# A hybrid decoder layer: more raw-weight buffers, background sums paced and placed anew

## The chip, the cores and the metric

The kernel runs on one core of a Trainium2 chip, in one launch. The metric is the device time of that launch in microseconds (us): the median of several executions of the same program. A profile is taken of one further execution.

## The reference

One layer on 512 tokens of width 1024, in float32. Cut to what matters here:

```python
xn = rms_norm(x, norm1_g)
proj = xn @ w_in                     # q, k, v, branch gates, conv inputs, merge gates
o_nsa = ...                          # compressed + selected + window attention
z = conv_b * conv3(conv_c * conv_x)  # short causal convolution
mixed = sigmoid(gate_a) * (o_nsa @ w_branch_a) + sigmoid(gate_b) * (z @ w_branch_b)
x = x + mixed @ w_out
h = rms_norm(x, norm2_g)
return x + square(relu(h @ w_up)) @ w_down
```

`w_up` is 1024 x 4096 and `w_down` 4096 x 1024.

## The kernel before

**Split products.** Every weight is used as a pair. ScalarE copies a raw chunk to a rounded `w_hi` (line 86), VectorE subtracts to get `w_lo` (line 88), and each product is three matmuls on TensorE (`mm3`, lines 229 to 231). The class `Weights` keeps a plan of all chunks (128 x 1024 floats, 512 KB, some smaller) in the order of use. A raw buffer (`w_raw`, three of them) is filled by a DMA on SyncE's queue (line 62). `split_step` issues the split in program order some chunks ahead of use. When a chunk is split, `load_to(ns + 2)` issues the load that reuses its buffer, so each load waits for the `w_lo` just issued, and whatever stands behind it on SyncE's queue waits too.

**Stages.** In order: the projections and attention; the merge (eight passes of four products, gates and branches); the output projection in two halves of 512 columns; and the feed-forward part in four groups, each an up stage (`up_group`) and a down stage (`st_down`). The second half of the output projection runs token chunk by token chunk (`tok_gemm` with `tok_outer`): 24 matmuls a chunk, then `o_second` (residual add, line 855; norm to `hn`, line 907), and inside the next chunk's matmuls `mid` calls `h_chunk`, which transposes `hn` on TensorE (line 917), copies it out on ScalarE and takes the remainder on VectorE (line 926).

**Feed-forward.** Each group multiplies in seven products instead of eight (block sums of the weights, in the manner of Strassen and Winograd). The products p1 to p7 of an up stage are written by `Quad`; VectorE forms the results (line 1025) and block sums (line 1069), and the pair for the down stage (line 1019). There are two such quads per group; quads 0 and 1 of the first group are interleaved, the other groups run them one after the other.

**Background sums.** The block sums of weights (`tu1` to `tu4` for an up stage, `td1` to `td4` for a down stage) are made ahead in DRAM, while other stages run. There are eight sets, `sums[0]` to `sums[7]`. `sums_by_dma` copies DRAM to DRAM on SyncE's queue (line 289), then accumulates on GpSimd's queue (line 293). `sums_by_dve` loads four pieces to buffers `z`, `oT`, `bg`, adds on VectorE (line 302, 128 x 1024) and stores (lines 305 to 316). `background(steps, pace)` hands over a list of steps, and `tick(us)` issues one each time the program's own estimate of elapsed time has grown by `pace`. Sets 0 to 2 are made by DMA at 4.95 in the first part, sets 3 to 6 by VectorE at 1.8 from the first merge pass on (100 steps), and set 7, needed in the last down stage, by DMA at 13.0 from the start of the up stage of the first group.

Of the kernel before, what the change touches and what calls it, by code (L numbers as in the profile page):

```python
# [6 lines left out]
F32 = mybir.dt.float32  # L7
# [6 lines left out]
P = 128  # L14
# [4 lines left out]
NT = S // P  # L19
# [13 lines left out]
C_ALL = 1484  # L33


class Weights:


    def __init__(self, nc, raw, hl, flat, plan):
        self.nc, self.raw, self.hl, self.flat = nc, raw, hl, flat  # L40
        self.plan = plan
        self.at = 0
        self.loaded = {}
        self.parts = {}
        self.nl = 0
        self.wide = 1 << 30
        self.home = {}
        self.step = 0
        self.ns = 0

# [15 lines left out]
    def split_step(self):  # L66


        nc, k = self.nc, self.ns
        if k >= len(self.plan):  # L70
            return
        if self.step == 0:
            self.load_to(k)
            pool = self.home.get(k, self.hl)
            hi = pool.tile([P, WMAX], F32R, name="w_hi", tag="w_hi")
            lo = pool.tile([P, WMAX], F32R, name="w_lo", tag="w_lo")
            self.parts[k] = (hi, lo)
        hi, lo = self.parts[k]
        t = self.loaded[k]
        n = t.shape[1]  # L80
        if k >= self.wide:
            v = slice(0, n)
        else:
            v = slice(0, n // 2) if self.step < 2 else slice(n // 2, n)
        if self.step % 2 == 0:
            nc.scalar.activation(hi[:, v], t[:, v], AF.Copy)  # L86
        else:
            nc.vector.tensor_tensor(lo[:, v], t[:, v], hi[:, v].bitcast(F32), ALU.subtract)  # L88
        self.step = (self.step + 1) % (2 if k >= self.wide else 4)
        if self.step == 0:  # L90
            self.loaded.pop(k)
            self.ns += 1
            self.load_to(self.ns + 2)

    def split_to(self, i):
        while self.ns <= min(i, len(self.plan) - 1):
# [7 lines left out]
def layer(tc, flat, sizes, x, cst, wck, wcv, g1, g2, out):  # L104
    nc = tc.nc
# [13 lines left out]

    top.enter_context(tc.manual_schedule())  # L120
    cp, close_cp = pool("cp")
    wraw, close_wraw = pool("wraw", 3)
    whl, close_whl = pool("whl", 4)
    xtp, close_xtp = pool("xtp")
    qkv, close_qkv = pool("qkv")
# [37 lines left out]

    xs = [sp.tile([P, DM], F32, name=f"x{c}") for c in range(NT)]
    g1b = sp.tile([P, DM], F32, name="g1b")
    cs = cp.tile([P, C_ALL], F32, name="cs")
    warm = cp.tile([P, 1], F32, name="warm")
    nc.vector.memset(warm, 1.0)
    nc.scalar.activation(warm, warm, AF.Sqrt)
# [4 lines left out]
    for b in range(2):  # L174
        nc.sync.dma_start(xs[0][:, b * 512 : b * 512 + 512], x[0:P, b * 512 : b * 512 + 512])
    nc.sync.dma_start(g1b, g1.partition_broadcast(P))
    nc.scalar.dma_start(cs[:, C_ID : C_ID + P], cst[:, C_ID : C_ID + P])
    W.load_to(1)
    load_x(1)
    W.load_to(2)  # L180
    wck_t = pre.tile([P, 16, HD], F32, name="wck_t")
    wcv_t = pre.tile([P, 16, HD], F32, name="wcv_t")

    ident = cs[:, C_ID : C_ID + P]
    junk = sp.tile([P, DM], F32, name="junk")
    st1 = cp.tile([P, NT], F32, name="st1")
    xh = xtp.tile([P, NKO, S], F32R, name="xh")
# [87 lines left out]
    for c in range(NT):  # L275
# [2 lines left out]
            v, v, q_ss[:, c, :].unsqueeze(2).to_broadcast([P, NH, HD]), ALU.mult  # L278
        )
    close_sp()  # L280
    zp, close_zp = pool("zp", side="right")
    cvp, close_cvp = pool("cvp", 2, side="right")

    def sums_by_dma(sets):

        for u in sets:
            for k, m in ((4, 0), (6, 1), (5, 2), (7, 3)):
                for h in u:
                    nc.sync.dma_start(h[k], h[m])
                    yield  # L290
            for k, m in ((4, 1), (6, 2), (5, 4), (7, 5)):
                for h in u:
                    nc.gpsimd.dma_start(h[k], h[m], accum_op=ALU.add)
                    yield
# [505 lines left out]
    for n in range(NKO):  # L800
# [20 lines left out]
        if n == 0:  # L821

            r = [t[:, k : k + 2, :].rearrange("p a t -> p (a t)") for t, k in
                 ((z, 0), (z, 2), (z, 4), (z, 6), (oT, 0), (oT, 2))]
            r += [bgp.tile([P, 1024], F32, name=f"bg{k}") for k in range(2)]
            background(sums_by_dve(sums[3:7], (r[:4], r[4:])), 1.8)
    for f in (close_gp, close_bp, close_xtp):
        f()

# [28 lines left out]
    def tok_gemm(ci, act, after, tok_outer, last=False, mid=None):  # L858
# [15 lines left out]
        else:  # L874
            for c in range(NT):
                parts = 2 if last and c == NT - 1 else 1
                for b in range(parts):
                    n = 512 // parts
                    ps = ps_acc.tile([P, 512], F32, name="acc", tag="acc")
                    for kp in range(4):  # L880
                        hi, lo = W.get(ci + kp)
                        for k in range(2):
                            ko = 2 * kp + k
                            w = slice(k * 512 + b * n, k * 512 + (b + 1) * n)
                            mm3(ps[:, :n], part(act, ko, c), (hi[:, w], lo[:, w]),
                                ko == 0, ko == NKO - 1)
                        tick(1.45 / parts)
                        if (c, kp) in ((2, 1), (2, 3), (3, 0), (3, 1)):
                            W.split_to(W.ns)
                        if kp == 2 and b == parts - 1 and c:  # L890
                            mid(c - 1)
                    if parts == 1:
                        after(c, ps)
                    else:
                        after(c, ps[:, :n], b * n, n)
# [48 lines left out]

    tok_gemm(ci + 4, (mh, ml), o_second, True, mid=o_mid)
    ci += 8
    background(sums_by_dma(sums[7:]), 13.0)
    close_wo()
    close_bgp()
    close_mp()  # L950
# [169 lines left out]
    def st_down(ci, last):  # L1120
# [30 lines left out]
        for ps, slot_, start, reads in (  # L1151
# [18 lines left out]
            else:  # L1170

                for j, o, n in ((0, 0, 512), (1, 0, 512)) if not last else (
                    (1, 0, 256), (0, 0, 512), (1, 256, 256)
                ):
                    for c in range(2):
                        ci += c
# [5 lines left out]

    for g in range(4):
        up_group(g)
        st_down(ci, g == 3)
        ci += 14
    for f in (close_gp2, close_hs, close_up, close_hp, close_ps_acc, close_ps_tr, close_ps_t, close_whl, close_wraw, close_cp, close_dr):
# [112 lines left out]
```

## Time and profile before

| quantity | value |
| --- | --- |
| median of 3 runs | 832.41 us (831.45 to 834.02) |
| the profiled execution | 837.87 us, span of the trace 836.0 us |
| TensorE busy | 798.0 us, 95% of the span, 4421 matmuls |
| VectorE busy | 585.8 us, 70% |
| ScalarE busy | 395.7 us, 47% |
| GpSimd busy | 88.5 us, 11% |
| mean granted TensorE clock | 0.988 |
| DMA, mean over the span | 206 GB/s |

The trace gives for each instruction its start from the span's begin, its duration, and the idle time of its engine just before it with the instruction that ended that idle time. An engine's name with a q (SPq, ACTq) is its queue of instructions that issue DMAs. The share of busy time is an average over stages that have different limits, so the rows below are taken by stage.

### The profile page before, as it was taken

What the parts mean: (1) busy time and instruction counts of PE and PEld (TensorE: products, weight loads), DVE (VectorE), ACT (ScalarE), POOL (GpSimd) and SP (SyncE); (2) the same over time, 40 slices, a digit from 0 to 9 for tenths busy, and PEclk for the clock granted to TensorE, in tenths of its full rate; (3) what the DMA queues carried; (4) which work ended last, traced back from release to release, by engine and by line L of the source; (5) the groups of instructions that cost most, each with busy time, mean ns of one, the idle gap of its engine ahead of it and who ended that gap; (6) DMA issues with size and microseconds to landing.
All of it is one profiled execution on the core that took longest, in us unless ns stands there. A gap on an engine that the chain in (4) does not pass through costs nothing.

```text
span 836.0 us, 11917 instructions
## 1 busy us (share of the span) xinstructions
PE 798.0 (95%) x4421; PEld 686.2 (82%) x4421; DVE 585.8 (70%) x1005; ACT 395.7 (47%) x714; POOL 88.5 (11%) x138
## 2 busy tenths in 40 slices
PE   5999989999999999999999887889989999999998
PEld 4898868888888888888888677878988899889986
DVE  6677887666666376566555677667588869967984
ACT  5454555455544362232222556663355446535641
POOL 0001553234224100000000000000000000000000
PEclk9999999999999999999999999979999999999999
DMA  8346668559568748988799654868887665565562
GB/s 311 130 124 199 131 138 201 170 129 193 158 191 169 152 154 268 336 295 267 275 319 375 242 181 135 208 197 261 247 221 204 208 204 188 179 199 190 178 221 107
DMA packets 49450, 172.56 MB, mean 206 GB/s; under 512 B 5616, under 2 KB 6000, under 8 KB 49392
## 3 DMA queue, kind: packets, MB, share of 16 engines
q1 hardware_dynamic: 43920, 152.33, 54.3%
q0 software_dynamic: 4608, 16.78, 12.9%
q10 hardware_dynamic: 864, 2.69, 0.9%
q8 instruction: 35, 0.57, 0.3%
q14 instruction: 23, 0.19, 0.1%
HBM read 152.90 MB, written 52.43 MB: 246 GB/s over the span
## 4 chain that ended last, share of the span: by engine, by line
PE 76%; DVE 10%; DMA 6%; ACT 5%; issue 2%; POOL 0%; SPq 0%; ACTq 0%; DVEq 0%; POOLq 0%
PE acc L229 14%; PE acc L230 13%; PE acc L231 13%; PE dacc L229 5%; PE dacc L230 5%; PE dacc L231 5%; DVE w_lo L88 3%; PE uacc L229 3%; PE uacc L230 3%; DMA w_raw<-w_flat 3%; PE uacc L231 3%; DMA w_raw<-tu 2%; PE ptu L685 2%; PE sc L638 2%; ACT w_hi L86 1%
## 5 line engine op out<-in xcount | busy, mean ns | idle before, releaser
L88 DVE TENSOR_TENSOR w_lo<-w_raw,w_hi 128x512 fp32r<-128x512 f32 (+3 forms) x268 | 234.1, 887 | 96.1 <-ACT w_hi L86 95.6
L86 ACT ACTIVATE w_hi<-w_raw 128x512 fp32r<-128x512 f32 (+3 forms) x268 | 201.7, 779 | 113.9 <-PE dacc L231 42.7
L229 PE MATMUL acc<-xh,w_hi 128*128 128x512 f32 x336 | 137.3, 409 | 0.0
L231 PE MATMUL acc<-xh,w_lo 128*128 128x512 f32 x336 | 131.6, 392 | 0.0
L230 PE MATMUL acc<-xl,w_hi 128*128 128x512 f32 x336 | 131.5, 391 | 0.0
L229 PE MATMUL dacc<-w_hi,uh 128*128 128x512 f32 (+1 forms) x228 | 88.2, 387 | 1.0 <-DVE x L1131 0.9
L230 PE MATMUL dacc<-w_lo,uh 128*128 128x512 f32 (+1 forms) x228 | 87.9, 386 | 0.0
L231 PE MATMUL dacc<-w_hi,ul 128*128 128x512 f32 (+1 forms) x228 | 87.9, 385 | 0.0
L231 PEld LDWEIGHTS acc<-xh,w_lo 128*128 128x128 f32 x336 | 63.1, 188 | 14.1
L229 PEld LDWEIGHTS acc<-xh,w_hi 128*128 128x128 f32 x336 | 63.2, 188 | 12.0 <-issue 3.3
L230 PEld LDWEIGHTS acc<-xl,w_hi 128*128 128x128 f32 x336 | 63.3, 188 | 7.9
L229 PE MATMUL uacc<-hA,w_hi 128*128 128x256 f32 x192 | 56.7, 295 | 9.9 <-DVE G L1025 9.9
L230 PE MATMUL uacc<-hA,w_hi 128*128 128x256 f32 x192 | 56.2, 292 | 0.0
L231 PE MATMUL uacc<-hA,w_lo 128*128 128x256 f32 x192 | 56.1, 292 | 0.0
L650 ACT ACTIVATE p<-p,nst 128x512 f32<-128x512 f32 (+2 forms) x48 | 29.6, 617 | 55.9 <-DVE nst L646 54.6
L229 PEld LDWEIGHTS dacc<-w_hi,uh 128*128 128x128 f32 x228 | 43.0, 188 | 10.4 <-issue 1.3
L231 PEld LDWEIGHTS dacc<-w_hi,ul 128*128 128x128 f32 x228 | 42.8, 188 | 8.7
L230 PEld LDWEIGHTS dacc<-w_lo,uh 128*128 128x128 f32 x228 | 43.0, 188 | 8.3
L229 PEld LDWEIGHTS uacc<-hA,w_hi 128*128 128x128 f32 x192 | 38.9, 203 | 10.6 <-DVE G L1025 6.9
L1131 DVE TENSOR_TENSOR x<-x,dacc 128x512 f32<-128x512 f32 (+1 forms) x57 | 36.7, 672 | 9.1 <-PE dacc L231 9.1
L691 DVE TENSOR_TENSOR pt<-ptu,pt 128x384 fp32r<-128x384 f32 (+1 forms) x48 | 28.8, 600 | 19.6 <-ACT pt L690 19.5
L666 POOL TENSOR_SCALAR p<-p,nst 128x512 f32<-128x512 f32 (+2 forms) x48 | 32.9, 693 | 88.3 <-DVE nst L664 43.3
(231 smaller groups left out, 1666.2 us busy)
## 6 DMA issues: line engine op xcount, KB each, us to landing
w_raw<-w_flat SPq DMA_DIRECT2D x110, 512.0 KB, 4.6
w_raw<-tu SPq DMA_DIRECT2D x32, 512.0 KB, 4.1
w_raw<-td SPq DMA_DIRECT2D x32, 512.0 KB, 4.4
tu<-w_flat SPq DMA_DIRECT2D x16, 512.0 KB, 6.1
td<-w_flat SPq DMA_DIRECT2D x16, 512.0 KB, 6.3
z<-w_flat SPq DMA_DIRECT2D x16, 512.0 KB, 6.7
tu<-w_flat POOLq DMA_DIRECT2D x8, 512.0 KB, 7.6
tu<-tu POOLq DMA_DIRECT2D x8, 512.0 KB, 9.4
```

The lines of the kernel that those rows point to most:

```text
L86: nc.scalar.activation(hi[:, v], t[:, v], AF.Copy)
L88: nc.vector.tensor_tensor(lo[:, v], t[:, v], hi[:, v].bitcast(F32), ALU.subtract)
L229: nc.tensor.matmul(ps, a[0], b[0], start=start, stop=False, **kw)
L230: nc.tensor.matmul(ps, a[0], b[1], start=False, stop=False, **kw)
L231: nc.tensor.matmul(ps, a[1], b[0], start=False, stop=stop, **kw)
L638: nc.tensor.matmul(ps[:, : b - a], QS[h][:, t], ks[h // 4][:, a:b], start=k == 0, stop=k == 1)
L650: later(1, lambda: nc.scalar.activation(p, p, AF.Exp, scale=-1.0, bias=mn, accum_out=sm))
L666: nc.gpsimd.tensor_scalar(p_of(u, k), p_of(u, k), nst[:, u % 4, 1, k : k + 1], 1.0, op0=ALU.mult, op1=ALU.mult,)
L685: nc.tensor.transpose(pt[:, n : n + P], p_of(u, c)[:, k * P : (k + 1) * P], ident)
L691: later(1, lambda: nc.vector.tensor_tensor(ptl[:, at], pt[:, :n], pth[:, at].bitcast(F32), ALU.subtract))
L1131: nc.vector.tensor_tensor(v, v, ps[:, o : o + n], op)
```

## The change

Parts of the diff, apart from names:

1. Five raw buffers instead of three, and a load depth that is 2 up to the end of the q projection and 4 from there on.
2. To make room, the table of constants `cs` moves to the pool that is freed before the merge; the identity for the transposes gets a small tile `ident`.
3. The sums on VectorE are paced at 1.55 instead of 1.8.
4. In the second half of the output projection the transposes of chunks 0 and 1 stand behind the next chunk's fourth weight chunk instead of behind its third; those of chunk 2 stay behind the third.
5. Set 7 starts after the up stage of the first group instead of before it, at 14.0 instead of 13.0, and its copies are issued on ScalarE's queue instead of SyncE's.
6. In the last product of the last group the 256-column pieces belong to the first accumulator instead of the second.

```diff
@@ class Weights
+        self.depth = 2
...
-            self.load_to(self.ns + 2)
+            self.load_to(self.ns + self.depth)
@@ layer
-    wraw, close_wraw = pool("wraw", 3)
+    wraw, close_wraw = pool("wraw", 5)
...
-    cs = cp.tile([P, C_ALL], F32, name="cs")
+    cs = qkv.tile([P, C_ALL], F32, name="cs")
+    ident = cp.tile([P, P], F32, name="ident")
...
-    nc.scalar.dma_start(cs[:, C_ID : C_ID + P], cst[:, C_ID : C_ID + P])
+    nc.scalar.dma_start(ident, cst[:, C_ID : C_ID + P])
...
     close_sp()
+    W.depth = 4
...
-    def sums_by_dma(sets):
+    def sums_by_dma(sets, copy=nc.sync.dma_start):
...
-                    nc.sync.dma_start(h[k], h[m])
+                    copy(h[k], h[m])
...
-            background(sums_by_dve(sums[3:7], (r[:4], r[4:])), 1.8)
+            background(sums_by_dve(sums[3:7], (r[:4], r[4:])), 1.55)
...
-                        if kp == 2 and b == parts - 1 and c:
+                        if kp == (2 if c == NT - 1 else 3) and b == parts - 1 and c:
                             mid(c - 1)
...
-    background(sums_by_dma(sums[7:]), 13.0)
...
-                    (1, 0, 256), (0, 0, 512), (1, 256, 256)
+                    (0, 0, 256), (1, 0, 512), (0, 256, 256)
...
     for g in range(4):
         up_group(g)
+        if g == 0:
+            background(sums_by_dma(sums[7:], nc.scalar.dma_start), 14.0)
         st_down(ci, g == 3)
```

Three places show what moves.

VectorE, second half of the output projection, from the norm of token chunk 0 to the add of chunk 2 (`x` is the residual, `st` the norm's sums, `hn` the normed chunk, `hA` its transposed remainder, `oT` and `bg` buffers of the background sums). Before:

```order
L907 SCALAR_TENSOR_TENSOR hn_4086<-x_0_4077,st_4091,g2b 128x1024
L302 TENSOR_TENSOR oT<-oT,bg_3090 128x1024
L926 TENSOR_TENSOR hA_4076<-ptr,hA_4075 128x2x2x128 x2
L302 TENSOR_TENSOR bg_3090<-bg_3090,oT 128x1024
L855 TENSOR_TENSOR x_1_4078<-acc,x_1_4078 128x512
L905 TENSOR_TENSOR st_4091<-st_4091 128x1
L192 TENSOR_SCALAR st_4091<-st_4091 128x1
L194 RECIPROCAL st_4091<-st_4091 128x1
L907 SCALAR_TENSOR_TENSOR hn_4087<-x_1_4078,st_4091,g2b 128x1024
L88 TENSOR_TENSOR w_lo<-w_raw,w_hi 128x1024
```

The same place in the changed kernel, to the add of chunk 2:

```order
L909 SCALAR_TENSOR_TENSOR hn_4102<-x_0_4093,st_4107,g2b 128x1024
L928 TENSOR_TENSOR hA_4092<-ptr,hA_4091 128x2x2x128 x2
L857 TENSOR_TENSOR x_1_4094<-acc,x_1_4094 128x512
L907 TENSOR_TENSOR st_4107<-st_4107 128x1
L193 TENSOR_SCALAR st_4107<-st_4107 128x1
L195 RECIPROCAL st_4107<-st_4107 128x1
L909 SCALAR_TENSOR_TENSOR hn_4103<-x_1_4094,st_4107,g2b 128x1024
L89 TENSOR_TENSOR w_lo<-w_raw,w_hi 128x1024 x2
L928 TENSOR_TENSOR hA_4092<-ptr,hA_4091 128x2x2x128 x2
L857 TENSOR_TENSOR x_2_4095<-acc,x_2_4095 128x512
```

The adds of the sums (line 302) are gone from here; they now stand ahead of the last splits of the first half. Two `w_lo` stand ahead of the second pair of `hA`, where one stood before.

TensorE at the transposes of chunk 1 (`ptr` from `hn1`), before:

```order
L229 MATMUL acc_4354<-w_hi_4267,mh_2929 128x512
L230 MATMUL acc_4354<-w_lo_4268,mh_2929 128x512
L231 MATMUL acc_4354<-w_hi_4267,ml_2930 128x512
L917 MATMUL ptr_4380<-cs_126,hn1_4087 128x128 x4
L917 MATMUL ptr_4388<-cs_126,hn1_4087 128x128 x4
L229 MATMUL acc_4354<-w_hi_4282,mh_2929 128x512
```

and now:

```order
L230 MATMUL acc_4363<-w_hi_4294,mh_2934 128x512
L231 MATMUL acc_4363<-w_lo_4295,mh_2934 128x512
L232 MATMUL acc_4363<-w_hi_4294,ml_2935 128x512
L919 MATMUL ptr_4400<-ident_127,hn1_4103 128x128 x4
L919 MATMUL ptr_4408<-ident_127,hn1_4103 128x128 x4
L230 MATMUL acc_4423<-w_hi_4191,mh_2934 128x512
```

The transposes moved from between two weight chunks of one accumulator to the seam between the accumulators of chunk 2 and chunk 3, six matmuls later.

SyncE's queue in the up stage of the first group, before (`w_raw` are loads of weights and of their sums, `td1_3` the first copies of set 7):

```order
L62 DMA w_raw_4590<-tu1_0_89 128x1024
L62 DMA w_raw_4627<-tu4_0_92 128x1024
L62 DMA w_raw_4672<-tu2_0_90 128x1024
L289 DMA td1_3_117<-w_flat 128x1024
L62 DMA w_raw_4705<-w_flat 128x1024
L62 DMA w_raw_4739<-tu3_0_91 128x1024
```

and now:

```order
L63 DMA w_raw_4446<-tu1_0_89 128x1024
L63 DMA w_raw_4540<-tu4_0_92 128x1024
L63 DMA w_raw_4595<-tu2_0_90 128x1024
L63 DMA w_raw_4632<-w_flat 128x1024
L63 DMA w_raw_4677<-tu3_0_91 128x1024
```

The eight copies of set 7 left this queue; on ScalarE's queue they stand between splits of the first group's down stage and the second group's up and down stages.

## Rows read from the trace of the kernel before

**Rows 1.** Page, busy time by engine over the span.

```profile
PE 798.0 (95%) x4421; PEld 686.2 (82%) x4421; DVE 585.8 (70%) x1005; ACT 395.7 (47%) x714; POOL 88.5 (11%) x138
```

**Rows 2.** Windows: output projection; up 1; up 2; down 3; up 4.

```profile
core 0: us, PE busy (x) PEld busy (x) DVE busy (x) ACT busy (x) POOL busy (x), PEclk, DMA share, GB/s
440.00:460.00 20.00, 20.00 (x88) 16.05 (x87) 11.36 (x15) 5.03 (x9) 0.00 (x0) 1.00 1.01 382
493.90:552.29 58.39, 46.33 (x345) 45.50 (x344) 40.51 (x49) 36.70 (x54) 1.62 (x2) 0.88 0.66 191
...
590.59:636.00 45.41, 42.24 (x337) 41.89 (x336) 33.26 (x40) 23.08 (x29) 2.44 (x3) 0.96 0.80 229
...
714.82:752.93 38.11, 38.11 (x170) 31.55 (x169) 29.18 (x36) 17.54 (x18) 0.00 (x0) 1.00 0.58 190
752.93:793.23 40.30, 40.30 (x337) 40.30 (x336) 34.92 (x42) 24.27 (x30) 0.00 (x0) 1.00 0.55 186
```

**Rows 3.** Timeline of TensorE, 460 to 836: instructions it was idle before, in brackets.

```profile
466.73 0.50 PE L230 MATMUL acc<-w_lo,mh 128*128 128x512 f32 x1 [0.69 <-DVE w_lo L88]
472.74 1.09 PE L917 MATMUL ptr<-cs,hn 128*128 128x128 f32 x8 [0.36 <-DVE hn L907]
480.99 1.07 PE L917 MATMUL ptr<-cs,hn 128*128 128x128 f32 x8 [1.54 <-DVE hn L907]
490.41 1.12 PE L917 MATMUL ptr<-cs,hn 128*128 128x128 f32 x8 [2.74 <-DVE hn L907]
...
517.57 0.39 PE L229 MATMUL uz<-hS,w_hi 128*128 128x256 f32 x1 [4.02 <-ACT p L1001]
...
547.01 0.58 PE L229 MATMUL uacc<-hA,w_hi 128*128 128x256 f32 x1 [6.70 <-DVE G L1025]
...
826.93 0.36 PE L229 MATMUL dacc<-w_hi,uh 128*128 128x256 f32 x1 [0.87 <-DVE x L1131]
```

**Rows 4.** Timeline of VectorE in the second half of the output projection.

```profile
475.53 0.69 DVE L926 TENSOR_TENSOR hA<-ptr,hA 128x512 fp32r<-128x512 f32 x1 [0.29 <-ACT hA L925]
476.14 1.22 DVE L302 TENSOR_TENSOR bg<-bg,oT 128x1024 f32<-128x1024 f32 x1
477.27 0.68 DVE L855 TENSOR_TENSOR x<-acc,x 128x512 f32<-128x512 f32 x1
...
480.76 1.22 DVE L88 TENSOR_TENSOR w_lo<-w_raw,w_hi 128x1024 fp32r<-128x1024 f32 x1
...
486.63 0.68 DVE L855 TENSOR_TENSOR x<-acc,x 128x512 f32<-128x512 f32 x1
```

**Rows 5.** Timeline of ScalarE, then of VectorE, 535 to 547.

```profile
535.07 1.06 ACT L86 ACTIVATE w_hi<-w_raw 128x1024 fp32r<-128x1024 f32 x1 [2.93 <-DMA w_raw<-tu]
...
536.16 1.23 DVE L88 TENSOR_TENSOR w_lo<-w_raw,w_hi 128x1024 fp32r<-128x1024 f32 x1 [3.30 <-ACT w_hi L86]
...
546.27 0.68 DVE L1025 TENSOR_TENSOR G<-p,uacc 128x512 f32<-128x512 f32 x1
```

**Rows 6.** Timeline of ScalarE, up stage of the second group.

```profile
594.60 1.06 ACT L86 ACTIVATE w_hi<-w_raw 128x1024 fp32r<-128x1024 f32 x1 [4.10 <-DMA w_raw<-w_flat]
...
607.08 1.06 ACT L86 ACTIVATE w_hi<-w_raw 128x1024 fp32r<-128x1024 f32 x1 [5.32 <-DMA w_raw<-w_flat]
```

**Rows 7.** The chain that ended last, 515 to 640: start, duration, what.

```profile
524.43 10.61 DMA w_raw<-tu
...
598.37 8.60 DMA w_raw<-w_flat
```

**Rows 8.** DMA issues by line: count, KB each, median us to landing.

```profile
bg<-w_flat SPq DMA_DIRECT2D x8, 512.0 KB, 7.7
```

**Rows 9.** Timelines of the queues: issues on ScalarE's, and a copy on SyncE's.

```profile
440.56 1.83 ACTq L845 DMA_DIRECT2D x<-x_in  x4
...
517.24 0.51 SPq L289 DMA_DIRECT2D td<-w_flat  x1
```

**Rows 10.** Timeline of VectorE, first half of the output projection.

```profile
455.61 1.22 DVE L302 TENSOR_TENSOR z<-z 128x1024 f32<-128x1024 f32 x1 [0.49 <-DMA z<-w_flat]
```

More of the change, by code (lines that the diff above doesn't have):

```diff
@@ L182, in layer @@
     wcv_t = pre.tile([P, 16, HD], F32, name="wcv_t")
-    ident = cs[:, C_ID : C_ID + P]
     junk = sp.tile([P, DM], F32, name="junk")
```

## The prediction

> **What bounds the kernel now.** I read the busy shares first, then the windows stage by stage, then TensorE's idle stretches, then what each of them waited for. TensorE is busy 798 of 836 us [rows 1], so all that can be won without less work is idle or slow TensorE time. The windows say where it lies [rows 2]. An up stage does the same 336 matmuls in every group; the last takes 40.30 us with TensorE full and its clock at 1.00, the second 45.41, the first 58.39 (the latter with eight transposes more, about 1 us). The down stage of the third group takes 38.11 us for 168 matmuls of 512 columns, 0.227 us each; I use 0.23 below, and 5.5 us for 24. Earlier than 460 us, apart from the start, TensorE is idle for a few us in the attention part, which the change does not touch. The waits in the part after 460 are in [rows 3]: four in the second half of the output projection (0.69, 0.36, 1.54, 2.74), two large ones in the first up stage (4.02 and 6.70), one at the end (0.87).
>
> **The output projection.** The change takes VectorE's last four adds of the sums out of this half (1.22 us each, one is in [rows 4]) and puts the transposes of chunks 0 and 1 six matmuls (1.4 us) later. I replay it.
> - The first wait, 0.69, ends on a `w_lo` that stood behind an add of 1.22; without the add it goes.
> - Chunk 0: its transposes started at 472.74, after 0.36 of waiting [rows 3]. Its `hn` is ready 0.7 earlier now, and TensorE arrives 0.36 + 0.69 earlier but has 1.4 more to do: no wait, start at 473.0.
> - Chunk 1: in program order its add (line 855) stands behind the two `hA` of chunk 0. The second of these ended 3.48 us after the transposes began (475.53 + 0.69 - 472.74), which gives 476.5; the background add that came next [rows 4] is gone. From the add's start to the next transposes it took 3.72 us (477.27 to 480.99), so 480.2. TensorE is there at 473.0 + 0.9 for the transposes + 5.5 = 479.4. It waits 0.8 instead of 1.54, and then has nothing left of chunk 2, where before 1.4 us of it remained.
> - Chunk 2: two `w_lo` of 1.22 now stand ahead of the two `hA` (0.65 each in a row). `hn` of chunk 1 ends just before 480.2, so the add starts at about 483.9. From add to transposes it was 3.78 (486.63 to 490.41), which gives 487.6 instead of 490.41: **2.8 us** earlier. TensorE, there at 480.2 + 0.9 + 18 x 0.23 = 485.2, still waits 2.4 us.
>
> So the norm's chain over VectorE and ScalarE is late next, and not all of the 5.33 us of waiting goes. Bounds: 1.4 (if the later transposes push back the add as much as they help once more) to 5.3. I take 2.8. Further on, to 517 us, the chain from the last norm to the 4.02 us wait runs over VectorE and ScalarE and no DMA ends a wait in it; it moves as a whole, and that wait stays.
>
> **The first up stage.** TensorE's wait of 6.70 us at 547.01 ends on VectorE's line 1025, 546.27 + 0.68 [rows 3, 5]. VectorE worked from 536.16 to there almost without a break, and before that stood 3.30 us for ScalarE, which stood 2.93 us for a raw chunk [rows 5]. That chunk's load took 10.61 us [rows 7], among the copies of set 7 (the first issued at 517.24 [rows 9]) and with only two loads ahead. Now four loads are ahead and set 7 starts after this stage. A load that is late by 2.93 is covered by two more chunks, each worth 24 x 0.12 = 2.9 us of TensorE's time in an up stage (40.30 / 336 = 0.12). So all 2.93 goes: **2.9 us**. The rest of the 6.70 is VectorE's own work and stays. Bounds: nothing, and 58.39 - 40.30 - 1 = 17 if all waits of the stage fell; it is near the low end because the 4.02 and the rest of the 6.70 end on compute, not on a load.
>
> **The second up stage.** ScalarE waits 4.10 and 5.32 us for raw chunks [rows 6], and a load takes 8.60 us [rows 7]. With three buffers a buffer comes round once in 8.6 + 1.06 + 1.23 = 10.9 us, 3.6 us a chunk, while TensorE uses one in 2.9. With five it is 10.9 / 5 = 2.2 us, so the stage is no longer bound by loads, even with set 7 now running beside it. Gain 45.41 - 40.30 = **5.1 us**. Bounds: nothing, and 5.1, since the last group has no such waits. I take the upper end: the loads would have to take over 12 us before five buffers don't keep up (5 x 2.9 - 2.3).
>
> **The end.** The first matmuls of the last product waited 0.87 us for the read of the second accumulator, which is read last [rows 3]. They now begin with the first accumulator, whose read is issued a half step earlier: **0.9 us**, between nothing and 0.9.
>
> **What costs nothing, and its cover.** The eight copies on ScalarE's queue hold it for 1.83 / 4 = 0.46 us each [rows 9], 3.7 us in all; ScalarE is busy 24 of 40 us in an up stage [rows 2], and the splits have the two added chunks in hand. Without that cover it is 3.7. In the Trainium skill, the page "DMA: Bandwidth & Descriptors", section "Issuing engines are not separate DMA queues", says that all queues end on the same DMA engines and that using several saves only the time to issue. By that rule the copies do not stop competing with the weights, and if they are what makes the loads late the second up stage keeps its loss (the first of the rivals). The quicker pace of the sums adds no instruction; it puts four adds more (4.9 us) ahead of the output projection's second half, where VectorE is idle 8.6 of 20 us [rows 2], and shortens the time that a load of the sums has. The constants' new place and the separate identity change no transfer on the path: 0. The deeper loads before the merge meet no wait of TensorE: 0.
>
> **Sum.** 2.8 + 2.9 + 5.1 + 0.9 = 11.7 us. The profiled execution took 837.87 us (836.0 of span and 1.9 around it), which makes 826.2. The median of the runs shown is 832.41, 5.5 below the profiled one; the waits are the same program's, so I take the 11.7 off the median: **820.7 us**.
>
> **The rivals.**
> - *The loads stay late.* The copies and the accumulations of set 7 move from the first up stage into the first down and second up stage, where they share the DMA engines with the weights, now from a second queue. For it: the share of the DMA engines is 0.80 in the second up stage and the rate only 229 GB/s, against 382 in the output projection [rows 2]. Against it: loads of 8.6 us fit five buffers. It keeps the 5.1: gain 6.6, 825.8 us.
> - *More falls than the load waits.* The four waits of the projection go altogether (2.5 more), and with shorter idle stretches the clock drops less: the mean granted clock of 0.88 in the first up stage [rows 2] is a quarter of 58 us at the 1.2 GHz level, mostly idle or just after the two long waits; 2.5 of it may come back. Gain 16.7, 815.7 us.
> - *It does not do what it says.* Every load still stands on SyncE's queue behind the `w_lo` that frees its buffer, and the sums' stores stand there too. If the order of that queue and not the depth makes the loads late, only the projection and the end win, less ScalarE's 3.7: near no change, 831 us.
> - *Slower.* The sums on VectorE starve. A buffer's next load is issued six steps before its add: 10.8 us at the old pace, 9.3 at the new. Such a load takes 7.7 us in the median [rows 8], and one was late at the old pace already, by 0.49 [rows 10]. VectorE works in order, so the splits and the gates stand behind a late add. The splits are two chunks ahead, which covers about one chunk, 5.5 us; so TensorE pays from a landing of 14.8 us on, once in each of eight jobs. Against it: the loads are far from that, and the first half of the projection gets less traffic. It decides from 14.8 + 11.7 / 8 = 16.3 us; at 17 it is 8 x 2.2 = 17.6 lost, 838.3 us.
>
> **How the numbers follow.** The forecast gets 0.62, loads that stay late 0.17, more 0.09, no change 0.07, slower 0.05. The range of 8 in 10 is 815 to 827: it takes in the two cases that lie beside the forecast and 1 us of spread around the late loads. About 0.3%, 2.5 us, is what a measurement can tell from no change. Faster by more: 0.62 + 0.17 + 0.09 = 0.88, of which I give 0.01 to no change for part gains that cancel: 0.87; within: 0.08; slower: 0.05.
>
> **What would show it.** Right: the second up stage at 40 to 41 us with no ScalarE wait for `w_raw`; in the first, one wait near 4 us as before and the second at 4 instead of 6.7; two waits for `hn` of about 0.8 and 2.4 before the feed-forward part; the first up stage begins about 3 us earlier; no wait at the last product. Wrong: loads of over 12 us in the second group, VectorE idle for `z`, `oT` or `bg` in the merge, matmuls there over 0.23 us, ScalarE idle behind its own DMA issues, or a new wait of TensorE in the first 460 us.

## The result and the profile after

The changed kernel takes 820.60 us (median of 4 runs, 819.86 to 821.24); the kernel before, on the same chip, 833.16 (831.45 to 834.02). The ratio is 0.9851, with a 95% interval of 0.9831 to 0.9872: 12.6 us less, where 11.7 were forecast, and 820.6 where 820.7 was (the forecast counts from 832.41, the median of before that was known then).

The profiled execution of the changed kernel took 820.94 us (span 819.2), close to its median; that of before took 837.87, 4.7 above its own. So the two traces differ by 16.9 us where the medians differ by 12.6, and part of what follows is how late the loads were in one execution of before. The page's line of busy shares, where TensorE goes from 95% [rows 1] to 97%:

```profile
PE 790.5 (97%) x4421; PEld 681.2 (83%) x4421; DVE 585.3 (71%) x1005; ACT 396.2 (48%) x714; POOL 88.2 (11%) x138
```

The windows that answer to [rows 2], with the same columns: the output projection, the first and second up stage, the third down stage, the fourth up stage.

```profile
440.00:460.00 20.00, 20.00 (x87) 16.10 (x86) 11.44 (x15) 5.02 (x9) 0.00 (x0) 1.00 0.95 356
489.21:543.78 54.57, 44.99 (x346) 44.38 (x345) 41.24 (x52) 36.54 (x55) 0.00 (x0) 0.91 0.44 144
581.88:621.68 39.80, 39.80 (x338) 39.79 (x337) 34.79 (x42) 24.27 (x30) 1.61 (x2) 1.00 0.91 263
699.58:737.68 38.10, 38.10 (x170) 31.54 (x169) 29.17 (x36) 17.52 (x18) 0.00 (x0) 1.00 0.60 195
737.68:777.48 39.80, 39.80 (x338) 39.79 (x337) 34.79 (x42) 24.27 (x30) 0.00 (x0) 1.00 0.56 185
```

The second up stage is full, though the DMA engines are busier there than before (0.91 against 0.80, 263 GB/s against 229). The fourth, which nothing in the change seemed to touch, is 0.5 us shorter. TensorE's idle stretches after 440 us, which answer to [rows 3]:

```profile
479.76 1.07 PE L919 MATMUL ptr<-ident,hn 128*128 128x128 f32 x8 [0.42 <-DVE hn L909]
486.91 1.06 PE L919 MATMUL ptr<-ident,hn 128*128 128x128 f32 x8 [1.89 <-DVE hn L909]
505.48 0.38 PE L231 MATMUL uacc<-hS,w_hi 128*128 128x256 f32 x1 [0.82 <-DVE hS L939]
512.52 0.47 PE L230 MATMUL uz<-hS,w_hi 128*128 128x256 f32 x1 [4.08 <-ACT p L1002]
538.79 0.58 PE L230 MATMUL uacc<-hA,w_hi 128*128 128x256 f32 x1 [4.69 <-DVE G L1026]
```

The waits of 0.69 and 0.36 in the projection and of 0.87 at the end are gone; 1.54 became 0.42, 2.74 became 1.89, 4.02 stayed (4.08), 6.70 became 4.69. ScalarE waits for no raw chunk in the second group. From the starts of the first matmuls, the stages (us, the two profiled executions):

| stage | before | after | less |
| --- | --- | --- | --- |
| output projection, to the first up stage | 55.00 | 50.18 | 4.82 |
| up 1 | 58.39 | 54.57 | 3.82 |
| down 1 | 38.30 | 38.10 | 0.20 |
| up 2 | 45.41 | 39.80 | 5.61 |
| down 2, up 3, down 3, up 4 | 157.23 | 155.80 | 1.43 |
| down 4 | 39.54 | 38.44 | 1.10 |

### The profile page after: what moved, and what is told of

Its sections match the earlier page's. It is cut to its first block, busy times and chain, and to the rows that moved or that the text cites. A ratio compares the mean times of both kernels' runs of the same rounds, so it can differ in the third digit from the quotient of the medians.

```text
span 819.2 us, 11917 instructions
## 1 busy us (share of the span) xinstructions
PE 790.5 (97%) x4421; PEld 681.2 (83%) x4421; DVE 585.3 (71%) x1005; ACT 396.2 (48%) x714; POOL 88.2 (11%) x138
## 4 chain that ended last, share of the span: by engine, by line
PE 86%; DVE 7%; ACT 4%; issue 1%; DMA 1%; POOL 0%; SPq 0%; ACTq 0%; DVEq 0%; POOLq 0%
PE acc L230 14%; PE acc L232 14%; PE acc L231 14%; PE dacc L230 6%; PE dacc L232 6%; PE dacc L231 6%; PE uacc L230 4%; PE uacc L231 4%; PE uacc L232 4%; PE ptu L687 2%; PE sc L640 2%; PE uz L230 2%; PE uz L231 2%; PE uz L232 2%; PE pv L711 1%
## 5 line engine op out<-in xcount | busy, mean ns | idle before, releaser
L230 PE MATMUL uacc<-hA,w_hi 128*128 128x256 f32 x192 | 55.4, 289 | 4.7 <-DVE G L1026 4.7
L231 PE MATMUL uacc<-hA,w_hi 128*128 128x256 f32 x192 | 55.2, 288 | 0.0
```

The lines of the kernel that those rows point to most:

```text
L230: nc.tensor.matmul(ps, a[0], b[0], start=start, stop=False, **kw)
L231: nc.tensor.matmul(ps, a[0], b[1], start=False, stop=False, **kw)
```

## The experiments

Each run was compared with the kernel before on the same chip; medians in us. The median of before was 833.16 in the result and lies between 834.81 and 835.52 beside these runs, so runs of different groups are best compared by their ratios.

| run | what it is | time | ratio to before, interval |
| --- | --- | --- | --- |
| again | before, unchanged | 834.65 | 1.0004 (0.9972 to 1.0036) |
| buffers_only | before + five buffers, depth 4 | 826.80 | 0.9903 (0.9871 to 0.9935) |
| no_buffers | after, three buffers, depth 2 | 835.23 | 1.0000 (0.9972 to 1.0028) |
| set7_old | after, set 7 as before | 821.77 | 0.9844 (0.9803 to 0.9885) |
| four_bufs | after, four buffers, depth 3 | 823.02 | 0.9879 (0.9843 to 0.9915) |
| pace_old | after, pace 1.8 | 824.50 | 0.9878 (0.9855 to 0.9900) |
| trans_old | after, transposes as before | 822.61 | 0.9856 (0.9835 to 0.9877) |
| norm_first | after, norm ahead of the copies | 822.25 | 0.9862 (0.9838 to 0.9886) |
| after_again | after, unchanged | 822.00 | 0.9843 (0.9812 to 0.9874) |
| chains | after, three reorderings | 814.34 | 0.9751 (0.9722 to 0.9780) |
| shift416 | after, `hA`, `uh`, `ul` moved | 825.28 | 0.9882 (0.9855 to 0.9910) |
| both | chains, `hA` moved alone | 814.31 | 0.9743 (0.9713 to 0.9773) |

**The kernel before, again.** No edit.

> The kernel before, unchanged, for a second profile. The profiled execution shown was 4.7 us above the median of its kernel. If that was one slow stage of this one execution, a second profile shows the same waits (projection 0.69, 0.36, 1.54, 2.74; first up stage 4.02 and 6.70; second up stage 45.4 us) and one stage shorter; if up stages of 40.30 against 39.80 us in the changed kernel come from the code, they are 40.3 here too; if from that execution, 39.8. Time 833 us.

834.65. Its third and fourth up stages take 40.30 us again, so the 39.80 of the changed kernel comes from the code. Its ten executions lie between 832.33 and 840.10, those of the changed kernel within 1.4. The trace has the same waits in the projection and the first up stage, and others at the loads: the second up stage takes 46.42 us instead of 45.41, the first down stage 39.92 instead of 38.30. With five buffers and nothing else of the change (the next run) nine executions lie within 3.2, with three buffers and all the rest twelve within 6.4. So the spread of before is mostly the loads', and a sum of waits from one execution is uncertain by some us.

**Only the buffers.**

```diff
-    wraw, close_wraw = pool("wraw", 3)
+    wraw, close_wraw = pool("wraw", 5)
...
     close_sp()
+    W.depth = 4
```

and the constants' new place, which makes room for them.

> The kernel before with five raw buffers and loads four ahead, nothing else of the change (the constants move, as they must). Theory, depth hides the late loads: the 2.93 in the first up stage and the 5.1 in the second go, 833.2 - 8.0 = 825.2 us, with the copies of set 7 still in their old place. Rival, the traffic of set 7 or the order of the queue makes the loads late whatever the depth: 831 to 833 us, and ScalarE's waits for raw chunks stay.

826.80 against 834.89 in this group: 8.1 us (5.4 to 10.8 by the interval), where the two load terms of the prediction make 8.0. The wait of 6.70 fell to 4.69 and the second up stage to 39.79; the projection's waits (0.67, 0.37, 1.56, 2.76) and the one at the end (0.87) stayed:

```profile
493.78:548.85 55.07, 45.49 (x345) 44.87 (x344) 40.33 (x49) 36.66 (x54) 1.62 (x2) 0.90 0.70 200
586.97:626.76 39.79, 39.79 (x337) 39.79 (x336) 34.77 (x42) 24.28 (x30) 2.44 (x3) 1.00 0.93 268
```

Set 7 still starts before the first up stage here, and its copies still stand on SyncE's queue: ScalarE waits for no raw chunk all the same, as long as there are five buffers.

**All but the buffers.**

```diff
-    wraw, close_wraw = pool("wraw", 5)
+    wraw, close_wraw = pool("wraw", 3)
...
-    W.depth = 4
+    W.depth = 2
```

> The changed kernel with three buffers and loads two ahead again. Theory: the first up stage keeps its gain of 2.9, since set 7 no longer runs in it, and the second up stage, with set 7 beside it, takes 45 to 46 us again: 820.6 + 5.5 = 826 us. Rival, the new place and queue of set 7 make the gain and the buffers add nothing: 821 us, second up stage 40 us.

835.23, no change: both expectations missed, by 9 and 14 us. The projection kept its gain (50.18 us to the first up stage), the end too (38.44), and so did the first up stage, as the theory said (54.63 us against 58.39 before). The second up stage took 43.73, less than the expected 45 to 46. What neither expectation had are the losses in the first down stage (41.18), the second (39.69) and the third up stage (44.83); they took the rest back. Set 7's transfers are issued from 557 to 672 us here, from 517 to 630 before, and ScalarE stood for raw chunks from 565 to 684; three of its 19 waits, and the windows of the first down, second up and third up stage:

```profile
575.77 1.06 ACT L87 ACTIVATE w_hi<-w_raw 128x1024 fp32r<-128x1024 f32 x1 [6.43 <-DMA w_raw<-td]
599.44 1.06 ACT L87 ACTIVATE w_hi<-w_raw 128x1024 fp32r<-128x1024 f32 x1 [4.82 <-DMA w_raw<-w_flat]
667.52 1.06 ACT L87 ACTIVATE w_hi<-w_raw 128x1024 fp32r<-128x1024 f32 x1 [4.62 <-DMA w_raw<-tu]
```

```profile
543.18:584.36 41.18, 38.34 (x170) 31.46 (x169) 27.40 (x32) 17.96 (x19) 1.61 (x2) 1.00 0.70 192
584.36:628.09 43.73, 40.50 (x338) 39.95 (x336) 33.42 (x40) 22.72 (x30) 1.93 (x3) 1.00 0.83 241
667.78:712.61 44.83, 41.85 (x338) 41.46 (x336) 35.88 (x43) 25.83 (x32) 0.81 (x1) 0.96 0.65 203
```

Before, up 3 took 40.30; here the last accumulations of set 7 lie beside it, and up 4, behind them, is full at 39.79. The raw chunks whose loads were issued from 557 to 680 us landed in 5.6 us in the median and 9.7 at most, those from 690 to 790, when set 7 was done, in 4.0 and 4.8. In the first up stage, where TensorE waits for VectorE anyway, late loads had cost 3.3 us at most (58.39 before, 55.07 with the buffers alone), less than the 5.0 of the third up stage here. That the move of set 7 is what took the gain back is read from this coincidence; three buffers with set 7 in its old place and the rest of the change weren't run, nor its new place with the copies on SyncE's queue, so place and queue are not told apart. The parts don't add: the buffers are worth 8.1 us alone and about 13 on top of the others (ratios of 1.0000 against 0.9851 and 0.9843), and the others nothing without them. In the Trainium skill, "DMA: Bandwidth & Descriptors", section "Issuing engines are not separate DMA queues" says that DMAs issued by ScalarE, SyncE and GpSimd all run on the same 16 DMA engines. These rows agree: with the copies on ScalarE's queue the loads on SyncE's come late all the same.

**Set 7 where it was,** with five buffers: ahead of the first up stage, at 13.0, on SyncE's queue.

```diff
+    background(sums_by_dma(sums[7:]), 13.0)
...
-        if g == 0:
-            background(sums_by_dma(sums[7:], nc.scalar.dma_start), 14.0)
```

> The changed kernel with set 7 as before: on SyncE's queue, at 13.0, from ahead of the first up stage. Theory: with five buffers the place does not matter, 820.6 to 822 us, no ScalarE wait for raw chunks. Rival, all queues share the DMA engines, so copies in the first up stage delay the loads that it cannot spare: 3 us more, 823.6 us, the 6.70 us wait of the first up stage back.

821.77, the changed kernel's time within the intervals; the second up stage takes 39.79, the wait that was 6.70 is 4.69 as in the changed kernel, and ScalarE waits for no raw chunk. With five buffers the move of set 7 is worth nothing that these runs can tell.

**Four buffers.**

```diff
-    wraw, close_wraw = pool("wraw", 5)
+    wraw, close_wraw = pool("wraw", 4)
...
-    W.depth = 4
+    W.depth = 3
```

> The changed kernel with four raw buffers and a depth of 3. By the prediction's formula a buffer comes round in 8.6 + 1.06 + 1.23 = 10.9 us, 2.7 us a chunk, still under the 2.9 us in which TensorE uses one: no ScalarE wait for a raw chunk that TensorE sees, time 820.6 to 821.5. Rival: it is the single late load, not the mean rate, that has to be covered; a further buffer covers one chunk (2.9 us) of the waits of up to 6.4 us that ScalarE had with three buffers, so that half of the 14.6 us between three and five stays: 825 to 828 us.

823.02, one of five executions at 829.54, the others 822.4 to 823.1; the changed kernel measured 820.60 and 822.00. That is 1.5 us above the expected range. In the trace the stages from the first down stage on are those of five buffers within 0.2 us each; 1.4 us went behind the wait of 1.74 near 115, where the clock fell (below). So the formula held, with little in hand; what happened in the execution of 829.54 isn't known. ScalarE now does stand for chunks, and TensorE doesn't notice; the longest:

```profile
577.80 1.06 ACT L87 ACTIVATE w_hi<-w_raw 128x1024 fp32r<-128x1024 f32 x1 [3.56 <-DMA w_raw<-w_flat]
```

**The old pace.**

```diff
-            background(sums_by_dve(sums[3:7], (r[:4], r[4:])), 1.55)
+            background(sums_by_dve(sums[3:7], (r[:4], r[4:])), 1.8)
```

> The changed kernel with the sums on VectorE paced at 1.8 again. By the prediction's step the last four adds (1.22 us each) come back into the second half of the output projection, one ahead of a `w_lo` and others ahead of the second `hA` and the next add, so the wait of about 0.7 near 466 and a wait of 2.5 to 3 before the last transposes come back: the first up stage starts 2.8 later by the sum, 4.7 later if the clock falls again as in the trace of before (493.9 against 489.2). Time 823.4 to 825.3 us. Rival: the adds were never what TensorE waited for, the transposes' place was; then 820.6.

824.50. The ratio, 0.9878, lies above the changed kernel's 0.9851 and 0.9843, but the intervals overlap, so the trace decides. TensorE's transposes of chunks 1 and 2:

```profile
482.08 1.06 PE L919 MATMUL ptr<-ident,hn 128*128 128x128 f32 x8 [0.43 <-DVE hn L909]
490.24 1.94 PE L919 MATMUL ptr<-ident,hn 128*128 128x128 f32 x8 [2.90 <-DVE hn L909]
```

A wait of 2.90 is back, and 0.68 at 468. From the first matmul of the projection to the up stage it is 53.61 us. That is 3.4 more than the 50.18 of the changed kernel's first trace, in which the clock stayed up behind the last wait, and 2.2 more than the 51.45 of its second (below), in which it fell as it did here; 4.7 and 2.8 were expected. So the adds were waited for, and the rival is out, but they carry less than the sum said.

**The old place of the transposes.**

```diff
-                        if kp == (2 if c == NT - 1 else 3) and b == parts - 1 and c:
+                        if kp == 2 and b == parts - 1 and c:
```

> The changed kernel with the transposes of chunks 0 and 1 behind the third weight chunk again, the pace still 1.55. The same replay, with the adds gone and the transposes 1.4 us earlier, gives waits that grow by about as much as the transposes start earlier, one `w_lo` less ahead of the second pair of `hA` of chunk 1: the first up stage within 0.5 us of 489.2, time 820.1 to 821.1. Rival: the later place carries part of the 4.7 us that the first up stage won; then it begins 1.4 us later or more (one step of six matmuls) and the time is 822 or more.

822.61, not to be told from the changed kernel by the time. In the trace the projection takes 52.47 us, 2.3 more than in the changed kernel's first trace and 1.0 more than in its second (below). The replay said within 0.5: it missed. The clock fell behind the last wait here as in the second trace, so the later place carries 1.0 at most and the clock the rest of the 2.3; the start of the last transposes, ahead of the fall, says 0.7 (table in the next section). The waits are 0.37, 0.44 and 1.98.

**The norm ahead of the copies.**

```diff
                     if parts == 1:
                         after(c, ps)
+                        if c:
+                            mid(c - 1)
```

with `mid` taken out of the matmuls of chunks 1 and 2.

> The changed kernel with one thing moved: in the second half of the output projection the residual add and the norm of a chunk are issued ahead of the copies and remainders of the transposes of the chunk before, not behind them; TensorE's order is the same. If the norm's chain over VectorE and ScalarE is what is late (the add of chunk 1 stands from 472.7, when its products are done, to 476.0 behind the two `hA`), `hn` comes 3 us earlier and the waits of 0.42 and 1.89 at the transposes go: the first up stage starts 2.3 us earlier, 818.3 us. Rival: the remainders, now behind the norm, are late for the sums of the first up stage, and what is won comes back as a longer wait at 508 (4.07 now): 820.6.

822.25: no gain. The two waits did go, but the edit also sends chunk 2 through `mid` a second time, behind the norm of chunk 3, which the expectation doesn't say. The transposes here are of chunk 2, and of chunk 2 again:

```profile
486.37 1.25 PE L921 MATMUL ptr<-ident,hn 128*128 128x128 f32 x8
489.87 1.09 PE L921 MATMUL ptr<-ident,hn 128*128 128x128 f32 x8 [0.84 <-DVE hA L930]
```

That puts 0.84 + 0.85 us on TensorE and about 1.4 on VectorE ahead of the first up stage, which took 57.17 us. So this run doesn't decide between its two expectations.

**The changed kernel, again.** No edit.

> The changed kernel once more, unchanged, as the measure for the other two of this group and for the spread of the changed kernel. If its time is set by its own instructions, 820.6 within 1.5 us, with the first up stage at 54.6 us and the second at 39.8. In three of the last four traces the clock fell to its lower level after the wait of 1.74 us at 114 and the rest began 1.4 us later, in the trace of the changed kernel it did not: if that falls by chance, medians of up to 822 are to be had from the same program.

822.00 (821.33 to 822.53), within the 1.5 us. Behind the wait at 114 the clock stayed up this time as well; it fell at another place. The stages are as in the first trace, but the projection took 51.45 us instead of 50.18 and the first up stage 55.23 instead of 54.57. The same wait, 1.88 us, stands ahead of the last transposes; the six matmuls behind them, in the first trace and in this one:

```profile
487.73:489.21 1.48, 1.48 (x10) 1.21 (x8) 1.48 (x3) 1.48 (x4) 0.00 (x0) 1.00 0.17 39
```

```profile
487.39:490.10 2.71, 2.71 (x9) 2.12 (x8) 2.54 (x5) 1.45 (x4) 0.00 (x0) 0.50 0.47 138
```

The granted clock is 1.00 in the one and 0.50, the 1.2 GHz level, in the other.

**Three reorderings.** The norm as above, with each chunk transposed once; in the first up stage the copy `p` ahead of two squarings on ScalarE, and the subtraction `G` ahead of a remainder `ul` on VectorE.

```diff
+                        if c in (1, 2):
+                            mid(c - 1)
...
-            later(2, lambda: self.square(d))
+            later(sq, lambda: self.square(d))
...
-        b.p2(24)
-        for f in (a.p5, a.p6, a.p3, a.p7, b.p5, a.p4, b.p6, b.p3, b.p7, b.p4):
+        b.p2(24, 10)
+        for f in (a.p5, a.p6, a.p3, a.p7, b.p5, a.p4, b.p6, lambda: b.p3(4), b.p7, b.p4):
```

> The changed kernel with three things reordered on VectorE and ScalarE and none on TensorE: the add and norm of chunks 1 and 2 ahead of the copies of the transposes of the chunk before (each chunk transposed once); in the first up stage the copy of the fifth product (`p`) ahead of two squarings on ScalarE; and the last subtraction (`G` from `p`) ahead of a remainder (`ul`) that waits for ScalarE. If what TensorE waits for after the change is the order of work on these two engines, the waits of 0.42 and 1.89 go, 4.08 falls to 1.7 (the copy 2.3 earlier) and 4.69 to 3.2 (the subtraction 1.5 earlier): 6 us, 6 us below the changed kernel of this group, 814.6 at 820.6. Rival: the amount of work on VectorE between the last norm and the third product is what counts; then the first two waits come back in the up stage and only 2 to 4 us are won, 817 to 819. If nothing is won, 820.6, the waits were only moved.

814.34, 7.7 us below the changed kernel in the same group, where 6 were expected. The copy `p` (20.8 us into the first up stage, which begins at 486.65; 22.7 in the changed kernel, 511.89 from 489.21) and TensorE's waits after 490 us:

```profile
507.44 0.57 ACT L1004 ACTIVATE p<-uz 128x512 f32<-128x512 f32 x1
```

```profile
503.47 0.38 PE L231 MATMUL uacc<-hS,w_hi 128*128 128x256 f32 x1 [0.88 <-DVE hS L941]
508.07 0.39 PE L230 MATMUL uz<-hS,w_hi 128*128 128x256 f32 x1 [1.64 <-ACT p L1004]
517.89 0.35 PE L230 MATMUL uacc<-hA,w_hi 128*128 128x256 f32 x1 [0.77 <-DVE G L1028]
532.52 0.39 PE L230 MATMUL uacc<-hA,w_hi 128*128 128x256 f32 x1 [3.06 <-DVE G L1028]
```

The waits ahead of the transposes are gone, 4.08 is 1.64 and 4.69 is 3.06, as expected; a new one is 0.77. The windows of this first up stage around 508 and to its end:

```profile
507.00:515.00 8.00, 6.90 (x56) 6.70 (x57) 7.37 (x8) 7.00 (x11) 0.00 (x0) 1.00 0.61 205
...
530.00:536.99 6.99, 4.47 (x24) 4.47 (x25) 5.03 (x6) 4.62 (x7) 0.00 (x0) 0.76 0.51 159
```

Behind 1.64 the clock stays at 1.00, where it was 0.72 in the changed kernel behind 4.08 (511 to 517 us). The last product takes 4.47 us from 532.52 to the end of the stage, against 4.99 from 538.79 in the changed kernel and 2.88 at the full clock. The waits that are gone or shorter make 5.5 us together (11.9 of idle time in the changed kernel, 6.4 here); the clock makes up the rest of the 7.7. What TensorE waits for after the change is thus the order of the work on VectorE and ScalarE, with TensorE's own order the same matmul for matmul, and this kernel beats both. The three reorderings were not run one by one.

**Another place for `hA`.**

```diff
+    gap, close_gap = pool("gap")
+    gap.tile([P, 104], F32, name="gap")
     hp_, close_hp = pool("hp")
```

> The changed kernel with 416 unused bytes per partition ahead of `hA` and the down stage's `uh` and `ul`, nothing else. In the change an up stage takes 39.80 us against 40.30 before although its instructions are the same: the four products that read `hS` take 2.82 us each instead of 2.88, the three that read `hA` 2.88 in both. `hS` stands at the same address in both, the weights moved, and their distance is 416 bytes (of 1024) now and 96 before; `hA` stands at distance 0 in both. If that distance sets the step between matmuls, the `hA` products fall to 2.82 as well and an up stage to 39.4: 1.3 us over the groups, and more if the down stage follows; 819.3 or less against the changed kernel of this group. Rival: the absolute place of the weights' buffers does it, or something else; then no stage changes.

825.28, 3.3 slower than the changed kernel. Down 2, down 3 and up 4:

```profile
624.53:663.74 39.21, 39.21 (x171) 31.54 (x170) 29.24 (x36) 17.43 (x18) 1.90 (x3) 1.00 0.91 256
703.16:742.35 39.19, 39.19 (x171) 31.54 (x169) 29.34 (x36) 17.50 (x18) 0.00 (x0) 1.00 0.58 191
742.35:781.77 39.42, 39.42 (x337) 39.42 (x336) 34.62 (x42) 24.27 (x30) 0.00 (x0) 1.00 0.57 183
```

Up 3 and up 4 fell to 39.42 as expected (every product 2.82 us), up 2 didn't (39.88), and the down stages rose by 1.0 to 1.1: `uh` and `ul` had moved by 416 bytes too.

**`hA` alone, with the three reorderings.** The 104 floats stand ahead of `hA` as in the run before; 152 more behind it put `uh` and `ul` 1024 bytes beyond their place.

```diff
     np_, close_np = pool("np")
+    gap2, close_gap2 = pool("gap2")
+    gap2.tile([P, 152], F32, name="gap2")
```

(ahead of `np`)

> The three reorderings (814.34) with the 416 bytes ahead of `hA`, and 608 further unused bytes behind it, so that `uh` and `ul` stand 1024 bytes beyond their place in the changed kernel, not 416. With 416 alone the up stages fell from 39.8 to 39.4 and the down stages rose from 38.1 to 39.2. If the up stage's gain goes with the place of `hA` and the down stage's loss with that of `uh` and `ul`, each to itself, this keeps the one without the other: up stages 39.4, down stages 38.1, 0.4 in each of four groups, 812.7. Rival: the loss comes with `hA`'s place as well (the residual behind it, which the down stage's adds read, has moved too): 39.2 in the down stages, 3.3 more than the gain, 817.

814.31, the same as without. Down 3 and up 4:

```profile
693.26:731.37 38.11, 38.11 (x170) 31.55 (x169) 29.18 (x36) 17.54 (x18) 0.00 (x0) 1.00 0.59 194
731.37:771.24 39.87, 39.87 (x337) 39.87 (x336) 34.73 (x42) 24.29 (x30) 0.00 (x0) 1.00 0.56 186
```

The down stage's loss went with the place of `uh` and `ul`: that half held. The up stages stayed at 39.87, all products at 2.85, with `hA`, `hS` and the split weights at the addresses that gave 39.42 in the run before. So the distance from `hA` to the weights alone doesn't set the step, and that half fell.

## Why the prediction was right

**The loads: right, with sizes that fit by luck.** The load terms, 2.9 + 5.1, are 8.0; the buffers alone gave 8.1 in the medians. The reason given, a buffer that comes round in 10.9 us against a chunk used in 2.9, is borne out from three sides: with three buffers waits, with four none that TensorE sees, with five none at all. That the sum fits so well is luck in part. The terms were read from an execution of before 4.7 us above its median, and at least 1.5 of the 8.1 are the shorter step of the matmuls (below), which that run has as well; that leaves 6.6 at most for the loads. And the 8.6 us in the formula is a late load. In the trace of before the raw chunks whose loads were issued from 515 to 640 us landed in 5.7 us in the median (10.6 at most); with 5.7 the formula gives (5.7 + 1.06 + 1.23) / 3 = 2.7 us a chunk, under 2.9, and three buffers would do. So the late loads are what the buffers have to cover. Within the terms one size was off: of the first up stage's 2.93 us for a late chunk, only 2.0 came off TensorE's long wait (6.70 to 4.69, where 3.8 was forecast). A small wait ahead of it, which the prediction doesn't have, went as well:

```profile
537.18 0.39 PE L229 MATMUL uacc<-hS,w_hi 128*128 128x256 f32 x1 [0.58 <-ACT u L1001]
```

The rest of the 3.8 us that this stage lost is steadier clock (mean 0.91 against 0.88) and the shorter step of the matmuls.

**The output projection: right in kind, mis-sized.** The replay can be read off without the clock at the start of the transposes of chunk 2, counted from the projection's first matmul:

| kernel | first matmul | transposes of chunk 2 | between |
| --- | --- | --- | --- |
| before | 438.90 | 490.41 | 51.51 |
| the replay | 438.90 | 487.6 | 48.7 |
| after, first trace | 439.03 | 486.91 | 47.88 |
| after, second trace | 438.65 | 486.54 | 47.89 |
| after, pace 1.8 | 440.40 | 490.24 | 49.84 |
| after, transposes as before | 439.26 | 487.83 | 48.57 |

The term of 2.8 measured 3.6 in both traces; half of the missing 0.8 was there at chunk 0, whose transposes began 33.67 us after the first matmul where the replay had 34.1. Of the 3.6 the adds carry 2.0 (the old pace) and the later place of the transposes 0.7 (the old place). What the whole stage won was 3.6 in the second trace and 4.8 in the first; the 1.2 between them is the clock, which fell behind the last wait before and in the second trace and happened not to in the first.

**The end: right.** 0.9 forecast; the wait is gone and the last stage is 1.1 us shorter (39.54 to 38.44).

**What costs nothing: with five buffers.** The copies on ScalarE's queue cost TensorE nothing (820.60 and 822.00 against 821.77 with the old place and queue). The prediction named the two added chunks as the cover for their issue and put 3.7 us on the change without it. The chunks were the cover for their traffic too: without them the loads came late, the first of the rivals, and the loss was about 13 us (835.23). The pace brought late loads of the sums, as the slower rival said, but not late enough for TensorE: this add stood 4.32 us for its load, which had been issued at 446.28, 9.3 us before.

```profile
455.58 1.23 DVE L304 TENSOR_TENSOR bg<-bg,bg 128x1024 f32<-128x1024 f32 x1 [4.32 <-DMA bg<-w_flat]
```

TensorE didn't idle there (the first window after), which fits the rival's own price: TensorE pays from a landing of 14.8 us on.

**What no step had.** The up stages' shorter step, 0.5 us in a stage: it came with the constants' new place, which was costed at nothing. It is in all kernels with that move, the one with three buffers included, and in none without it; the move was not run by itself. Over the three groups behind the first it makes 1.5 us, more than the 0.9 that the forecast was short of. So the total is nearer than its parts: the loads were worth less than forecast, the projection 0.8 to 2.0 more, and this step was not in the sum. That they cancel is luck.

## What to carry to other kernels

Count buffers by the time one takes to come round over the time in which one is used, and leave a buffer in hand. The time round is the landing of a late load under the traffic of that stage, not of the median one, plus the work that frees the buffer. With five buffers the place of the background transfers then cost nothing here; with three their new place came with the loss of all that the other edits had won. When loads no longer bound a stage, look for the in-order engine on which the instruction that TensorE waits for stands behind work that nobody waits for: here three such reorderings, without any change on TensorE, were worth 7.7 us. And compare kernels that differ in one part by the trace of the stage as well as by the median: the executions of the kernel before differed by more than most parts are worth. Where the clock may fall, compare two traces in which it did the same.

## What the runs showed of the hardware

- **The step between matmuls depends on where tiles lie.** The same 24 matmuls of 256 columns took 2.88, 2.85 or 2.82 us (products of an up stage: 2.88 throughout before; 2.88 for `hA` and 2.82 for `hS` after; 2.85 with both gaps), and those of 512 columns 5.44, or 5.60 with `uh` and `ul` moved by 416 bytes and 5.44 again at 1024. Which address decides in an up stage stays open: the same `hA`, `hS` and weights gave 2.82 in two groups of one kernel and 2.85 in another group of it and in the next kernel.
- **Whether the clock falls behind a short wait differs between executions of one program.** Behind the wait of 1.74 us at 114 it stayed at 1.00 in both traces of the changed kernel and fell to 0.50, the 1.2 GHz level, in that of four buffers (in 3 of all 14 traces). Behind 1.87 to 1.90 ahead of the last transposes it fell in two traces and stayed in four (one of each in the two windows above). The length of the wait alone doesn't decide: behind 1.98, 2.74 and 2.90 at that place it fell, and in the first down stage with three buffers it stayed behind 2.84, as this wait and the 2 us behind it show. What decides isn't known from these runs. The fall ahead of the first up stage cost 1.2 us in six matmuls (2.71 against 1.48).

```profile
578.83 0.47 PE L230 MATMUL dacc<-w_hi,uh 128*128 128x512 f32 x1 [2.84 <-DVE x L1132]
```

```profile
578.83:580.83 2.00, 2.00 (x9) 1.67 (x10) 1.53 (x2) 1.50 (x2) 0.00 (x0) 1.00 0.74 195
```

- **The changed kernel is steadier.** Its nine executions lie within 2.7 us (819.86 to 822.53); those of before lie within 7.2 in one group of nine (832.07 to 839.25) and within 11.2 in one of 26 (830.33 to 841.52).
